# One PSUM tile of three banks for all scores, one minimum and one exponential per head in the even mixer, and norms moved to VectorE

## The chip, the cores and the metric

The kernel runs on one core of a Trainium2 chip. The metric is device time in microseconds (us) for one execution; lower is better. Engines are written as in the profile: PE is TensorE (PEld its weight loads), DVE is VectorE, ACT is ScalarE, POOL is GpSimd, SP is SyncE, whose queue issues most transfers.

## The reference, cut to what matters

The program is two blocks behind each other on 512 tokens of width 1024, all in float32. Block 1 has two layers of latent attention (8 heads, called MLA here) beside a dilated attention, then a norm. Block 2 has an even mixer (attention over 512 own and 256 context keys, beside a multi-scale pool), a hierarchical mixture of 16 experts (moe), an odd mixer and a second moe. The two attentions whose scores the change touches:

```python
# MLA: 8 heads, 4 blocks of 128 queries, 512 keys
s = (qn . k_nope + qr . k_rope) * scale
p = jax.nn.softmax(s, axis=-1)
# even mixer: 8 query heads on 2 key heads, keys = context (256) and own (512)
k_all = jnp.concatenate([kc, k], axis=1)
s = jnp.einsum('bqkgd,bskd->bkgqs', q, k_all) * (HEAD_DIM ** -0.5)
p = jax.nn.softmax(s, axis=-1).astype(v.dtype)
o = jnp.einsum('bkgqs,bskd->bqkgd', p, v_all)
# norms in front of each layer
y = x * rsqrt(mean(x * x) + eps) * g        (block 2: * (1 + scale) + shift)
```

## The kernel before

Float32 products run on PE as three matmuls of a split operand: weights arrive by SP in `wraw` tiles, `split_to` (L403, L404) makes a rounded part `whi` on ACT and a rest `wlo` on DVE, and `mm3` (L352 to L354) issues the three matmuls. All sums land in PSUM, which has eight banks of 128x512 floats. `bank` hands them out as buffers of four tags: `s` (scores, two buffers), `mm` (projections and everything else, three), `pt` (transposes, two) and `av` (values, one). Each buffer is a tile of its own, and the program's builder puts semaphore waits on an instruction by the tiles that it reads and writes.

**Block 1** (span 0 to 955 us, one half for each layer). A layer's order of work is written out by hand: `unit(u)` for u from 0 to 66 issues the scores of unit u (L846 for MLA, 32 units; L825 and L833 for the dilated heads), then the transposes of the probabilities of unit u-2 (L866), and every eighth time the values. `weave` deals a list of fill steps between the units: projections (`fm`, whose sums are taken from PSUM by `block` on ACT, L570 and L574, or by `pair`, L625 and L627, `tile`, L640, and `query`, `key`, L694), gates (`gate`: L650 on ACT, L651 on DVE) and output projections (`wout`, L670 on DVE). For an MLA score DVE takes the row minimum (L848), ACT the exponential with its sum (`softmax`, L805), DVE the reciprocal and the scaling (L807, L808). DVE carries also the columns of the later blocks' modulation (L992, 1.2 us apiece).

**Layer-1 norms** (490 to 515 us): per 128 tokens ACT sums squares (L514), POOL multiplies with the gain (L515), DVE makes the reciprocal root in steps of one column (L386 to L399), ACT scales (L521), PE transposes.

**Even mixer** (955 to 1212 us): after norms and projections 32 units, two per pair of heads and block of 128 queries. `scores(u)` puts 512 own keys in an `s` bank (L1341) and 256 context keys in an `mm` bank (L1343), each as two matmuls; DVE takes two minima and their minimum (L1346 to L1348), ACT two exponentials (L1350, L1351), DVE adds the two sums, takes the reciprocal and scales (L1352 to L1354). `transposed(u-2)` (L1361) turns six pieces through two `pt` banks; `copy` takes turns between ACT (L368, the 512 wide) and DVE (L370, the 256 wide). `values` (L1373) follows every second unit. The fills are pool steps, further queries and the first half of the output projection.

**The moe** (1250 to 1424, 1660 to 1825 us) takes gate and up products of an expert in an `s` bank (`up`, read at L1774 to L1776) and the down product in `mm` banks (L1877, read by DVE at L1879). Its order of instructions is set by the builder's scheduler, not by hand. Behind the first moe come the passages' norms (`added`, L1974 to L1983, and `normed`, L1986), where POOL multiplies for three of four token blocks.

Of the kernel before, what the change touches and what calls it, by code (L numbers as in the profile page):

```python
# [9 lines left out]
F32 = mybir.dt.float32  # L10
# [4 lines left out]
AF = mybir.ActivationFunctionType  # L15
ALU = mybir.AluOpType
AX = mybir.AxisListType
# [4 lines left out]
P = 128  # L22
# [250 lines left out]
class K:  # L273
    def __init__(self, tc, ins, sb, ps, dr):
        self.tc, self.nc, self.I, self.sb, self.ps, self.dr = tc, tc.nc, ins, sb, ps, dr
        self.pool = sb
        self.extra = self.late = None
        self.rate = 0
        self.two = None
        self.tail = None  # L280
        self.of = {}
        self.mod = {}
        self.v4 = ("v4", 10)
        self.n = 0
        self.flip = 0

    def nm(self, s):
        self.n += 1
# [30 lines left out]
            rest(i, a)  # L319
            a, b = b, first(i + 2) if i < 2 else None  # L320

    def bank(self, tag, dt=F32):
        bufs = {"mm": 3, "s": 2, "pt": 2, "av": 1}[tag]
        return self.ps.tile([P, 512], dt, tag=tag, bufs=bufs, name=self.nm("ps" + tag))


    def raw(self, src, off, n):
# [125 lines left out]
def block1_layer(k, L, x, hT):  # L453
# [55 lines left out]
    if L:  # L509
        us, rss = {}, {}  # L510

        def square(i):
            u, ss = us[i], rss[i] = t([P, D], "v4", 10), t([P, 1], "ss", 2)
            nc.scalar.activation(u, x[:, i, :], AF.Square, scale=float(D ** -0.5), accum_out=ss)  # L514
            nc.gpsimd.tensor_tensor(u, x[:, i, :], gB, ALU.mult)  # L515

        def rms_(i):
            return k.rsqrt_steps(rss[i], 1, lambda rs: rss.update({i: rs}))

        def turned(i):  # L520
            nc.scalar.activation(us[i], us[i], AF.Copy, scale=rss[i])  # L521
            return k.norm_steps(us[i], hT, i)

        with k.tc.manual_schedule(engines={ENG.PE, ENG.SP, ENG.Pool, ENG.Activation, ENG.DVE}):
# [616 lines left out]
def even_mixer(k, x, rows):  # L1141
# [45 lines left out]
    nc.sync.dma_start(ic, I["pool_ic"].to_broadcast([P, 64]))  # L1187
    psc = t([P, 4], "psc", 1)
    nc.sync.dma_start(psc, I["psc"])
    for b in range(4):  # L1190
        v.tensor_scalar(psc[:, b : b + 1], psc[:, b : b + 1], 0.5 ** (b + 1), None, op0=ALU.mult)


    T = [t([P, 640], "T", 4) for _ in range(4)]
# [106 lines left out]
        pooled[b] = wp  # L1301

    def pool_mix(b):
        if b % 2 == 0:
            cats[2 + b // 2] = new_cat(k)
        cat = cats[2 + b // 2]
        y = k.bank("mm")
        nc.tensor.matmul(y, pw[:, b * P : (b + 1) * P], pooled[b], start=True, stop=True)
        hi, lo = cat[0][:, b % 2, :], cat[1][:, b % 2, :]
        nc.scalar.activation(hi, y, AF.Copy, scale=psc[:, b : b + 1])  # L1310
        v.scalar_tensor_tensor(lo, y, psc[:, b : b + 1], hi.bitcast(F32), op0=ALU.mult, op1=ALU.subtract)
# [24 lines left out]
    def scores(u):  # L1336
        hp, i, e = u // 8, u % 8 // 2, u % 2
        g, cs = hp // 2, slice(i * P, (i + 1) * P)
        sx, sc = k.bank("s"), k.bank("mm")
        for part in range(2):  # L1340
            nc.tensor.matmul(sx, Qs[(hp, e)][:, cs], Kx[g][part], start=part == 0, stop=part == 1)  # L1341
        for part in range(2):
            nc.tensor.matmul(sc[:, 0:256], Qs[(hp, e)][:, cs], Kc[g][part], start=part == 0, stop=part == 1)  # L1343
        mn = t([P, 3], "mn3", 3)
        l = t([P, 3], "l3", 3)
        v.tensor_reduce(mn[:, 0:1], sx, AX.X, ALU.min)  # L1346
        v.tensor_reduce(mn[:, 1:2], sc[:, 0:256], AX.X, ALU.min)
        v.tensor_tensor(mn[:, 2:3], mn[:, 0:1], mn[:, 1:2], ALU.min)  # L1348
        pr = prs[u] = t([P, 768], "pr", 3)
        nc.scalar.activation(pr[:, 0:512], sx, AF.Exp, scale=-1.0, bias=mn[:, 2:3], accum_out=l[:, 0:1])  # L1350
        nc.scalar.activation(pr[:, 512:768], sc[:, 0:256], AF.Exp, scale=-1.0, bias=mn[:, 2:3], accum_out=l[:, 1:2])  # L1351
        v.tensor_tensor(l[:, 2:3], l[:, 0:1], l[:, 1:2], ALU.add)  # L1352
        v.reciprocal(l[:, 2:3], l[:, 2:3])
        v.tensor_scalar(pr, pr, l[:, 2:3], None, op0=ALU.mult)  # L1354

    def transposed(u):
        PT = PTs[u] = t([P, 6, P], "PT", 4)
        for nk, o in ((4, 0), (2, 4)):
            pt = k.bank("pt")
            for j in range(nk):  # L1360
                nc.tensor.transpose(pt[:, j * P : (j + 1) * P], prs[u][:, (o + j) * P : (o + j + 1) * P], ident)  # L1361
            k.copy(PT[:, o : o + nk, :], pt[:, 0 : nk * P].rearrange("p (j q) -> p j q", j=nk))

    def values(u):

# [4 lines left out]
        for kt in range(6):  # L1370
            vv = V[:, kt, g * 64 : g * 64 + 64] if kt < 4 else ckv[:, kt * P - 256 + g * 64 : kt * P - 192 + g * 64]
            for e in range(2):
                nc.tensor.matmul(k.av[e * 64 : e * 64 + 64, cs], vv, PTs[u - 1 + e][:, kt, :], start=kt == 0, stop=kt == 5)  # L1373
        if i == 3:
            if hp % 2 == 0:
                cats[hp // 2] = new_cat(k, hp == 2)
# [26 lines left out]
    for g in range(2):  # L1403
# [11 lines left out]
        [q(3), mix(2), mix(3)] + wout(3),  # L1415
        wout(0) + [(1.3, lambda: router(k, 0))],
    )
    for w, fill in enumerate(fills):
        n = 8 if w < 3 else 12
        weave([lambda u=u: unit(u) for u in range(8 * w, 8 * w + n)], fill)  # L1420
    k.tail = wout2(k, I["mo"][0], 1, cats[1], x, g1B)


# [105 lines left out]
def moe(k, L, x, tables, out):  # L1529
# [444 lines left out]
    def added(i):  # L1974
# [5 lines left out]
            v.tensor_tensor(x[:, i, ns], acc, x[:, i, ns], ALU.add)  # L1980
            yield
        nc.scalar.activation(t([P, D], "y", 4), x[:, i, :], AF.Square, scale=float(D ** -0.5), accum_out=ss[:, i : i + 1])
        (nc.gpsimd if i else v).tensor_tensor(us[i], x[:, i, :], A1, ALU.mult)  # L1983

    def normed(i):
        v.scalar_tensor_tensor(us[i], us[i], rss[i], sh1, op0=ALU.mult, op1=ALU.add)  # L1986
# [120 lines left out]
```

## Time and profile before

| | us |
|---|---|
| three runs | 1845.24, 1846.01, 1849.75 |
| median | 1846.01 |
| profiled execution | 1847.55 |
| its span | 1845.8 |
| mean granted clock of PE | 0.961 of full speed |
| busy: PE / DVE / ACT / POOL | 1696.8 / 1329.8 / 769.9 / 273.4 |

The profile is of one execution; a row of the timeline gives start, duration, engine, line and operands of an instruction, and in brackets how long its engine had been idle before it and who ended that. Line numbers are those of the kernel before; in the changed kernel the same code stands some lines lower (`mm3` L362 to L364, the MLA score L855, its exponential L814, the transposes L875, the even mixer's scores L1352, its exponential L1357, the moe's down product L1884 and its reader L1886).

### The profile page before, as it was taken

To read this page: it belongs to the slowest core of one execution; us is meant where nothing else is said; L and a number is where in the kernel's file an instruction comes from. 1 tells how busy PE (TensorE), PEld (TensorE's weight loads), DVE (VectorE), ACT (ScalarE), POOL (GpSimd) and SP (SyncE) were. 2 spreads that over 40 slices of the span, in tenths; PEclk is the share of its full clock that TensorE was granted. 3 is DMA by queue.
4 is the path that set the end of the run, shared out by engine and by line. 5 is a ranking of instruction groups with operands and counts; after the bars stand their busy time and mean duration, and the time that the engine had idled before them with its cause. 6 is when DMAs were issued, how large, how long until landed. Compare 5 with 4: busy or idle time off the path is not lost. (4 is left out here: it accounts for less than half of the span.)

```text
span 1845.8 us, 25749 instructions
## 1 busy us (share of the span) xinstructions
PE 1696.8 (92%) x9542; PEld 1325.3 (72%) x9542; DVE 1329.8 (72%) x2519; ACT 769.9 (42%) x1345; POOL 273.4 (15%) x239
## 2 busy tenths in 40 slices
PE   7999999999799999999997888978999799969996
PEld 6877777886697777778776766856665687756663
DVE  5577779876646776566677888889876775589774
ACT  4444333343344533333443545544554322245552
POOL 0000000000200000000003552023221122142221
PEclk9999999999899999999998889988999899979998
DMA  5345565664024455565403223058995553169983
GB/s 177 122 137 159 152 203 179 215 191 127 20 86 121 147 153 149 172 189 154 146 27 111 78 82 115 8 199 295 334 345 145 197 184 92 42 252 308 345 291 75
DMA packets 87588, 300.99 MB, mean 163 GB/s; under 512 B 18982, under 2 KB 20822, under 8 KB 79264
## 3 DMA queue, kind: packets, MB, share of 16 engines
q1 hardware_dynamic: 72224, 273.97, 44.8%
q0 software_dynamic: 10704, 19.79, 4.7%
q10 hardware_dynamic: 4528, 5.51, 1.1%
q8 instruction: 78, 1.28, 0.3%
q14 instruction: 54, 0.44, 0.1%
HBM read 282.33 MB, written 24.96 MB: 166 GB/s over the span
## 5 line engine op out<-in xcount | busy, mean ns | idle before, releaser
L403 ACT ACTIVATE whi<-wraw 128x1024 fp32r<-128x1024 f32 (+2 forms) x166 | 171.8, 1036 | 341.6 <-PE psmm L353 210.8
L404 DVE TENSOR_TENSOR wlo<-wraw,whi 128x1024 fp32r<-128x1024 f32 (+2 forms) x166 | 203.1, 1225 | 104.4 <-ACT whi L403 95.8
L352 PE MATMUL psmm<-big,whi 128*128 128x512 f32 x672 | 271.8, 404 | 1.6 <-ACT e L1289 1.6
L353 PE MATMUL psmm<-big,whi 128*128 128x512 f32 x672 | 265.7, 395 | 0.0
L354 PE MATMUL psmm<-big,wlo 128*128 128x512 f32 x672 | 265.6, 395 | 0.0
L992 DVE CUSTOM_DVE_ANT_0 wraw<-wraw,sB 128x1024 f32<-128x1024 f32 x96 | 116.9, 1221 | 93.8 <-DMA wraw<-in_mw_dram 93.6
L352 PE MATMUL psmm<-whi,big 128*128 128x256 f32 (+2 forms) x496 | 165.6, 334 | 1.0 <-ACT big L403 1.0
L353 PE MATMUL psmm<-wlo,big 128*128 128x256 f32 (+2 forms) x496 | 161.1, 325 | 4.4 <-DVE wlo L404 4.4
L354 PE MATMUL psmm<-whi,big 128*128 128x256 f32 (+2 forms) x496 | 160.2, 323 | 2.5 <-DVE big L404 2.4
L354 PEld LDWEIGHTS psmm<-big,wlo 128*128 128x128 f32 x672 | 126.4, 188 | 30.8
L352 PEld LDWEIGHTS psmm<-big,whi 128*128 128x128 f32 x672 | 126.6, 188 | 29.9 <-ACT e L1289 1.8
L353 PEld LDWEIGHTS psmm<-big,whi 128*128 128x128 f32 x672 | 126.7, 189 | 27.7
L1877 PE MATMUL psmm<-wraw,hs 128*128 128x512 f32 x256 | 122.0, 618 | 5.5 <-ACT hs L1869 3.5
L603 POOL DMA_DIRECT2D qk<-rope x40 | 20.6, 517 | 660.9 <-DVE rope L601 254.1
L353 PEld LDWEIGHTS psmm<-wlo,big 128*128 128x128 f32 x496 | 112.7, 227 | 5.5 <-DVE wlo L404 5.3
L354 PEld LDWEIGHTS psmm<-whi,big 128*128 128x128 f32 x496 | 112.0, 226 | 3.4 <-DVE big L404 3.4
L352 PEld LDWEIGHTS psmm<-whi,big 128*128 128x128 f32 x496 | 112.0, 226 | 2.1 <-ACT big L403 1.6
L352 PE MATMUL pss<-whi,xTh 128*128 128x512 f32 x256 | 104.7, 409 | 2.1 <-ACT xTh L403 2.1
L354 PE MATMUL pss<-whi,xTl 128*128 128x512 f32 x256 | 102.2, 399 | 1.7 <-DVE xTl L404 1.3
L353 PE MATMUL pss<-wlo,xTh 128*128 128x512 f32 x256 | 103.4, 404 | 0.0
L866 PEld LDWEIGHTS pspt<-c_ident,pr 128*128 128x128 f32 x512 | 60.1, 141 | 48.1 <-issue 28.5
L404 DVE TENSOR_TENSOR wlo<-bigm,whi 128x1024 fp32r<-128x1024 f32 x64 | 77.9, 1223 | 17.8 <-ACT whi L403 16.3
(381 smaller groups left out, 3619.1 us busy)
## 6 DMA issues: line engine op xcount, KB each, us to landing
wraw<-in_mw_dram SPq DMA_DIRECT2D x96, 512.0 KB, 3.7
big<-in_me_dram SPq DMA_DIRECT2D x32, 1024.0 KB, 7.9
bigm<-in_me_dram SPq DMA_DIRECT2D x32, 1024.0 KB, 9.2
wraw<-in_me_dram SPq DMA_DIRECT2D x64, 512.0 KB, 8.2
wraw<-in_wqk_dram SPq DMA_DIRECT2D x48, 512.0 KB, 3.9
wraw<-in_wv_dram SPq DMA_DIRECT2D x24, 512.0 KB, 4.6
wraw<-in_ow_dram SPq DMA_DIRECT2D x20, 512.0 KB, 3.7
wraw<-in_wg_dram SPq DMA_DIRECT2D x16, 512.0 KB, 3.9
```

The lines of the kernel that those rows point to most:

```text
L352: mm(out, lhs[0], rhs[0], start=first, stop=False)
L353: mm(out, lhs[0], rhs[1], start=False, stop=False)
L354: mm(out, lhs[1], rhs[0], start=False, stop=last)
L403: self.nc.scalar.activation(hi, src, AF.Copy)
L404: (sub or self.nc.vector).tensor_tensor(lo, src, hi.bitcast(F32), ALU.subtract)
L603: nc.gpsimd.dma_start(tiles[b][48:80, :], R[j][32 * (b % 4) : 32 * (b % 4) + 32, :])
L866: nc.tensor.transpose(pt[:, j * P : (j + 1) * P], hd.pr[i][:, j * P : (j + 1) * P], ident)
L992: nc.vector.tensor_tensor_reduce(w, w, sB, 1.0, 0.0, ALU.mult, ALU.add, mf[:, j : j + 1])
L1877: nc.tensor.matmul(acc, hs[:, c * P : (c + 1) * P], w[:, c * 512 : (c + 1) * 512], start=c == 0, stop=c == 1)
```

## The change

One tile `wide` of three adjacent banks is allocated once and kept for the whole program. `bank("s")` hands out its first and third bank in turn. `bank("mm")` has two buffers of its own and outside the even mixer's units hands out the middle bank of `wide` as every third. In the even mixer's units a pair of heads shares the three banks: the first head has 512 own and 256 context keys in columns 0 to 767, the second 256 context and 512 own keys in columns 768 to 1535, so that one minimum and one exponential of 768 columns serve a head, the adds of partial results go, and the order of the pieces in `values` is rotated for the second head. Both copies of turned probabilities are on ACT. The scaling of `psc` goes into `pool_mix`. The layer-1 norms take one DVE instruction in place of POOL's multiply and ACT's scaling, and the passages' norms multiply on DVE alone.

```diff
--- before.py
+++ after.py
@@ -283,6 +283,8 @@
         self.v4 = ("v4", 10)
         self.n = 0
         self.flip = 0
+        self.wide = ps.tile([P, 3, 512], F32, name="wide")
+        self.turns, self.middle = {"s": 2, "mm": -1}, True
 
     def nm(self, s):
         self.n += 1
@@ -319,9 +321,17 @@
             rest(i, a)
             a, b = b, first(i + 2) if i < 2 else None
 
-    def bank(self, tag, dt=F32):
-        bufs = {"mm": 3, "s": 2, "pt": 2, "av": 1}[tag]
-        return self.ps.tile([P, 512], dt, tag=tag, bufs=bufs, name=self.nm("ps" + tag))
+    def bank(self, tag):
+
+        if tag == "s":
+            self.turns["s"] ^= 2
+            return self.wide[:, self.turns["s"], :]
+        if tag == "mm" and self.middle:
+            self.turns["mm"] = (self.turns["mm"] + 1) % 3
+            if self.turns["mm"] == 2:
+                return self.wide[:, 1, :]
+        bufs = {"mm": 2, "pt": 2, "av": 1}[tag]
+        return self.ps.tile([P, 512], F32, tag=tag, bufs=bufs, name=self.nm("ps" + tag))
 
 
     def raw(self, src, off, n):
@@ -512,13 +522,12 @@
         def square(i):
             u, ss = us[i], rss[i] = t([P, D], "v4", 10), t([P, 1], "ss", 2)
             nc.scalar.activation(u, x[:, i, :], AF.Square, scale=float(D ** -0.5), accum_out=ss)
-            nc.gpsimd.tensor_tensor(u, x[:, i, :], gB, ALU.mult)
 
         def rms_(i):
             return k.rsqrt_steps(rss[i], 1, lambda rs: rss.update({i: rs}))
 
         def turned(i):
-            nc.scalar.activation(us[i], us[i], AF.Copy, scale=rss[i])
+            nc.vector.scalar_tensor_tensor(us[i], x[:, i, :], rss[i], gB, op0=ALU.mult, op1=ALU.mult)
             return k.norm_steps(us[i], hT, i)
 
         with k.tc.manual_schedule(engines={ENG.PE, ENG.SP, ENG.Pool, ENG.Activation, ENG.DVE}):
@@ -1187,8 +1196,6 @@
     nc.sync.dma_start(ic, I["pool_ic"].to_broadcast([P, 64]))
     psc = t([P, 4], "psc", 1)
     nc.sync.dma_start(psc, I["psc"])
-    for b in range(4):
-        v.tensor_scalar(psc[:, b : b + 1], psc[:, b : b + 1], 0.5 ** (b + 1), None, op0=ALU.mult)
 
 
     T = [t([P, 640], "T", 4) for _ in range(4)]
@@ -1301,6 +1308,7 @@
         pooled[b] = wp
 
     def pool_mix(b):
+        v.tensor_scalar(psc[:, b : b + 1], psc[:, b : b + 1], 0.5 ** (b + 1), None, op0=ALU.mult)
         if b % 2 == 0:
             cats[2 + b // 2] = new_cat(k)
         cat = cats[2 + b // 2]
@@ -1336,22 +1344,19 @@
     def scores(u):
         hp, i, e = u // 8, u % 8 // 2, u % 2
         g, cs = hp // 2, slice(i * P, (i + 1) * P)
-        sx, sc = k.bank("s"), k.bank("mm")
-        for part in range(2):
-            nc.tensor.matmul(sx, Qs[(hp, e)][:, cs], Kx[g][part], start=part == 0, stop=part == 1)
-        for part in range(2):
-            nc.tensor.matmul(sc[:, 0:256], Qs[(hp, e)][:, cs], Kc[g][part], start=part == 0, stop=part == 1)
-        mn = t([P, 3], "mn3", 3)
-        l = t([P, 3], "l3", 3)
-        v.tensor_reduce(mn[:, 0:1], sx, AX.X, ALU.min)
-        v.tensor_reduce(mn[:, 1:2], sc[:, 0:256], AX.X, ALU.min)
-        v.tensor_tensor(mn[:, 2:3], mn[:, 0:1], mn[:, 1:2], ALU.min)
+
+        row = k.wide.rearrange("p b n -> p (b n)")
+        sx, sc = row[:, e * 1024 : e * 1024 + 512], row[:, 512 + e * 256 : 768 + e * 256]
+        for out, keys_ in ((sx, Kx), (sc, Kc)):
+            for part in range(2):
+                nc.tensor.matmul(out, Qs[(hp, e)][:, cs], keys_[g][part], start=part == 0, stop=part == 1)
+        src = row[:, e * 768 : e * 768 + 768]
+        mn, l = t([P, 1], "mn3", 3), t([P, 2], "l3", 3)
+        v.tensor_reduce(mn, src, AX.X, ALU.min)
         pr = prs[u] = t([P, 768], "pr", 3)
-        nc.scalar.activation(pr[:, 0:512], sx, AF.Exp, scale=-1.0, bias=mn[:, 2:3], accum_out=l[:, 0:1])
-        nc.scalar.activation(pr[:, 512:768], sc[:, 0:256], AF.Exp, scale=-1.0, bias=mn[:, 2:3], accum_out=l[:, 1:2])
-        v.tensor_tensor(l[:, 2:3], l[:, 0:1], l[:, 1:2], ALU.add)
-        v.reciprocal(l[:, 2:3], l[:, 2:3])
-        v.tensor_scalar(pr, pr, l[:, 2:3], None, op0=ALU.mult)
+        nc.scalar.activation(pr, src, AF.Exp, scale=-1.0, bias=mn, accum_out=l[:, 0:1])
+        v.reciprocal(l[:, 1:2], l[:, 0:1])
+        v.tensor_scalar(pr, pr, l[:, 1:2], None, op0=ALU.mult)
 
     def transposed(u):
         PT = PTs[u] = t([P, 6, P], "PT", 4)
@@ -1359,7 +1364,7 @@
             pt = k.bank("pt")
             for j in range(nk):
                 nc.tensor.transpose(pt[:, j * P : (j + 1) * P], prs[u][:, (o + j) * P : (o + j + 1) * P], ident)
-            k.copy(PT[:, o : o + nk, :], pt[:, 0 : nk * P].rearrange("p (j q) -> p j q", j=nk))
+            nc.scalar.activation(PT[:, o : o + nk, :], pt[:, 0 : nk * P].rearrange("p (j q) -> p j q", j=nk), AF.Copy)
 
     def values(u):
 
@@ -1370,7 +1375,7 @@
         for kt in range(6):
             vv = V[:, kt, g * 64 : g * 64 + 64] if kt < 4 else ckv[:, kt * P - 256 + g * 64 : kt * P - 192 + g * 64]
             for e in range(2):
-                nc.tensor.matmul(k.av[e * 64 : e * 64 + 64, cs], vv, PTs[u - 1 + e][:, kt, :], start=kt == 0, stop=kt == 5)
+                nc.tensor.matmul(k.av[e * 64 : e * 64 + 64, cs], vv, PTs[u - 1 + e][:, (kt + 2 * e) % 6, :], start=kt == 0, stop=kt == 5)
         if i == 3:
             if hp % 2 == 0:
                 cats[hp // 2] = new_cat(k, hp == 2)
@@ -1415,9 +1420,11 @@
         [q(3), mix(2), mix(3)] + wout(3),
         wout(0) + [(1.3, lambda: router(k, 0))],
     )
+    k.middle = False
     for w, fill in enumerate(fills):
         n = 8 if w < 3 else 12
         weave([lambda u=u: unit(u) for u in range(8 * w, 8 * w + n)], fill)
+    k.middle = True
     k.tail = wout2(k, I["mo"][0], 1, cats[1], x, g1B)
 
 
@@ -1980,7 +1987,7 @@
             v.tensor_tensor(x[:, i, ns], acc, x[:, i, ns], ALU.add)
             yield
         nc.scalar.activation(t([P, D], "y", 4), x[:, i, :], AF.Square, scale=float(D ** -0.5), accum_out=ss[:, i : i + 1])
-        (nc.gpsimd if i else v).tensor_tensor(us[i], x[:, i, :], A1, ALU.mult)
+        v.tensor_tensor(us[i], x[:, i, :], A1, ALU.mult)
 
     def normed(i):
         v.scalar_tensor_tensor(us[i], us[i], rss[i], sh1, op0=ALU.mult, op1=ALU.add)
```

Three places show how the built program's PE rows change. Behind a row in brackets stand the engines on whose semaphores it waits; `wide` is the new tile, `pss`, `psmm`, `pspt` buffers of the tags, `pr` probabilities.

PE in block 1, an MLA score, the transposes of the unit two before it, and the first product of a fill step; before:

```order
L846 MATMUL pss_1044<-qk_815,qk_801 128x512 [waits Activation_49]
L866 MATMUL pspt_1053<-c_ident,pr_948 128x128 [waits DVE_49,PE_49]
L866 MATMUL pspt_1053<-c_ident,pr_948 128x128 x3
L352 MATMUL psmm_1059<-whi_993,big_77 128x256
L353 MATMUL psmm_1059<-wlo_994,big_77 128x256
L354 MATMUL psmm_1059<-whi_993,big_78 128x256
```

and now:

```order
L855 MATMUL wide<-qk_808,qk_794 128x512 [waits Activation_49]
L875 MATMUL pspt_1038<-c_ident,pr_935 128x128 [waits PE_49]
L875 MATMUL pspt_1038<-c_ident,pr_935 128x128 x3
L362 MATMUL wide<-whi_979,big_78 128x256 [waits Activation_49]
L363 MATMUL wide<-wlo_980,big_78 128x256
L364 MATMUL wide<-whi_979,big_79 128x256
```

The order of the rows stays, but the fill step's first product, which goes to the middle bank and waited for nothing, now waits for ACT.

PE in the even mixer, the scores of units 0 and 1 and, behind a fill step, of unit 2; before:

```order
L1341 MATMUL pss_9658<-Kx_9519,Q_9549 128x512 [waits DVE_49,Activation_49]
L1341 MATMUL pss_9658<-Kx_9520,Q_9549 128x512 [waits DVE_49]
L1343 MATMUL psmm_9659<-Kc_9513,Q_9549 128x256
L1343 MATMUL psmm_9659<-Kc_9514,Q_9549 128x256
L1341 MATMUL pss_9675<-Kx_9519,Q_9552 128x512 [waits DVE_49]
L1341 MATMUL pss_9675<-Kx_9520,Q_9552 128x512
L1343 MATMUL psmm_9676<-Kc_9513,Q_9552 128x256
L1343 MATMUL psmm_9676<-Kc_9514,Q_9552 128x256
...
L1341 MATMUL pss_9735<-Kx_9519,Q_9549 128x512 [waits Activation_49]
L1341 MATMUL pss_9735<-Kx_9520,Q_9549 128x512
L1343 MATMUL psmm_9736<-Kc_9513,Q_9549 128x256 [waits Activation_49]
L1343 MATMUL psmm_9736<-Kc_9514,Q_9549 128x256
```

and now:

```order
L1352 MATMUL wide<-Kx_9304,Q_9334 128x512 [waits DVE_49,Activation_49]
L1352 MATMUL wide<-Kx_9305,Q_9334 128x512 [waits DVE_49]
L1352 MATMUL wide<-Kc_9298,Q_9334 128x256
L1352 MATMUL wide<-Kc_9299,Q_9334 128x256
L1352 MATMUL wide<-Kx_9304,Q_9337 128x512 [waits Activation_49]
L1352 MATMUL wide<-Kx_9305,Q_9337 128x512
L1352 MATMUL wide<-Kc_9298,Q_9337 128x256
L1352 MATMUL wide<-Kc_9299,Q_9337 128x256
...
L1352 MATMUL wide<-Kx_9304,Q_9334 128x512 [waits Activation_49]
L1352 MATMUL wide<-Kx_9305,Q_9334 128x512
L1352 MATMUL wide<-Kc_9298,Q_9334 128x256
L1352 MATMUL wide<-Kc_9299,Q_9334 128x256
```

The scores of units 0 and 1 waited apart for engines that had prepared their operands; now unit 1 waits for ACT, and behind the fill step one wait stands for the three banks.

PE in the first moe, in its steady part: turned inputs of an expert (L1759, now L1766), down products (L1877, now L1884), turned hidden values (L1867, now L1874) and the first gate and up product of the next expert (L352, now L362); before:

```order
L1867 MATMUL pspt_12519<-c_ident,pr_12427 128x128
L1759 MATMUL pspt_12545<-c_ident,xg_11252 128x128 [waits DMASW2_49,PE_49]
L1759 MATMUL pspt_12545<-c_ident,xg_11252 128x128 x3
L1877 MATMUL psmm_12529<-wraw_12525,hs_12522 128x512 [waits DMAHW1_49,Activation_49]
L1877 MATMUL psmm_12529<-wraw_12525,hs_12522 128x512
L1877 MATMUL psmm_12533<-wraw_12526,hs_12522 128x512 [waits DMAHW2_49]
L1877 MATMUL psmm_12533<-wraw_12526,hs_12522 128x512
L1759 MATMUL pspt_12552<-c_ident,xg_11252 128x128 [waits PE_49]
L1759 MATMUL pspt_12552<-c_ident,xg_11252 128x128 x3
L352 MATMUL pss_12559<-whi_12563,xTh_12543 128x512 [waits Activation_49]
```

and now:

```order
L1766 MATMUL pspt_12034<-c_ident,xg_10847 128x128 [waits DMASW1_49,PE_49]
L1766 MATMUL pspt_12034<-c_ident,xg_10847 128x128 x3
L1884 MATMUL psmm_12022<-wraw_12016,hs_12012 128x512 [waits DMAHW6_49,Activation_49]
L1884 MATMUL psmm_12022<-wraw_12016,hs_12012 128x512
L1884 MATMUL wide<-wraw_12015,hs_12012 128x512 [waits DMAHW5_49,DVE_49]
L1884 MATMUL wide<-wraw_12015,hs_12012 128x512
L1766 MATMUL pspt_12041<-c_ident,xg_10847 128x128 [waits PE_49]
L1766 MATMUL pspt_12041<-c_ident,xg_10847 128x128 x3
L1874 MATMUL pspt_12095<-c_ident,pr_12005 128x128 [waits DVE_49,PE_49]
L1874 MATMUL pspt_12095<-c_ident,pr_12005 128x128
L362 MATMUL wide<-whi_12051,xTh_12032 128x512 [waits DVE_49,Activation_49]
```

The transposes of the hidden values come ahead of the next expert's products instead of behind them, and both the second down product and those products wait for DVE.

## Rows read from the trace of the kernel before

**Rows 1.** Windows: busy us (instructions) by engine, PE's clock, DMA share, GB/s.

```profile
90.00:250.00 160.00, 158.89 (x735) 118.52 (x734) 115.75 (x210) 67.37 (x129) 3.27 (x6) 1.00 0.51 149
...
1057.00:1100.00 43.00, 34.09 (x176) 26.98 (x175) 36.58 (x73) 18.82 (x45) 25.21 (x22) 0.80 0.14 40
1100.00:1150.00 50.00, 44.84 (x309) 35.34 (x307) 41.11 (x94) 27.54 (x65) 14.54 (x10) 0.97 0.34 122
1250.00:1424.00 174.00, 167.35 (x738) 115.02 (x738) 144.21 (x203) 93.06 (x128) 42.91 (x29) 0.98 0.85 292
```

**Rows 2.** Timeline around an MLA score at 111.6: start, duration, engine, line, operands.

```profile
111.62 1.02 PE L846 MATMUL pss<-qk,qk 96*128 96x512 f32 x2
...
111.95 1.21 DVE L992 CUSTOM_DVE_ANT_0 wraw<-wraw,sB 128x1024 f32<-128x1024 f32 x1
...
112.84 0.36 PE L352 MATMUL psmm<-whi,big 128*128 128x256 f32 x1
...
113.47 0.69 DVE L848 TENSOR_REDUCE mn<-pss 128x1 f32<-128x512 f32 x1
...
114.26 0.69 ACT L805 ACTIVATE pr<-pss,mn 128x512 f32<-128x512 f32 x1 [0.54 <-DVE mn L848]
```

**Rows 3.** Timeline around the first MLA score: the score and the gate's last reader.

```profile
92.89 1.02 PE L846 MATMUL pss<-qk,qk 96*128 96x512 f32 x2
...
95.06 0.69 DVE L651 SCALAR_TENSOR_TENSOR gc<-gc,psmm 128x512 f32<-128x512 f32 x1
```

**Rows 4.** Timeline around a dilated score: the score and the copy that reads a projection.

```profile
919.78 0.66 PE L825 MATMUL pss<-k,qk 64*32 64x256 f32 x16
...
920.61 0.58 ACT L571 ACTIVATE k<-psmm 128x512 f32<-128x512 f32 x1
```

**Rows 5.** Line L574, copies of a projection: duration ns min/median/max.

```profile
L574 ACT ACTIVATE qk<-psmm x40: 571/578/598, 165.5 to 914.6; 128x512 f32<-128x512 f32 x40
```

**Rows 6.** Groups, 1054 to 1210: busy us, mean ns, idle before and releaser.

```profile
L1350 ACT ACTIVATE pr<-pss,mn 128x512 f32<-128x512 f32 x32 | 22.0, 686 | 32.6 <-DVE mn L1348 29.0 <-DVE rs_yn L399 2.8 <-DVE PT L370 0.8
L1346 DVE TENSOR_REDUCE mn<-pss 128x1 f32<-128x512 f32 x32 | 21.9, 683 | 7.9 <-PE pss L1341 7.8
...
L1351 ACT ACTIVATE pr<-psmm,mn 128x256 f32<-128x256 f32 x32 | 14.9, 465 | 0.0
...
L1352 DVE TENSOR_TENSOR l<-l 128x1 f32<-128x1 f32 x32 | 13.3, 416 | 7.0 <-ACT pr L1351 6.6
L1347 DVE TENSOR_REDUCE mn<-psmm 128x1 f32<-128x256 f32 x32 | 13.3, 414 | 0.0
L370 DVE COPY PT<-pspt 128x256 f32<-128x256 f32 x32 | 13.2, 414 | 0.2
...
L1348 DVE TENSOR_TENSOR mn<-mn 128x1 f32<-128x1 f32 x32 | 8.1, 252 | 0.0
```

**Rows 7.** Timeline of the layer-1 norms: POOL's multiply and root steps.

```profile
490.25 2.40 POOL L515 TENSOR_TENSOR v<-x,v 128x1024 f32<-128x1024 f32 x1 [44.66 <-ACT v L514]
...
491.10 1.56 DVE L393 SCALAR_TENSOR_TENSOR rs_u<-rs_y,rs_h 128x1 f32<-128x1 f32 x1
...
493.38 0.21 DVE L393 SCALAR_TENSOR_TENSOR rs_u<-rs_y,rs_h 128x1 f32<-128x1 f32 x1
```

**Rows 8.** Timeline in the first moe: a down product's reader and PE's next product.

```profile
1308.51 0.75 DVE L1879 SCALAR_TENSOR_TENSOR y<-psmm,ws,mv 128x512 f32<-128x512 f32 x1 [0.31 <-PE psmm L1877]
...
1308.66 0.47 PE L352 MATMUL pss<-whi,xTh 128*128 128x512 f32 x1
```

**Rows 9.** Windows around two gaps on PE, at 1586 and 307.

```profile
1585.00:1588.50 3.50, 1.65 (x8) 1.03 (x7) 2.99 (x2) 0.00 (x0) 2.44 (x1) 1.00 0.00 0
1588.50:1591.90 3.40, 3.40 (x10) 2.62 (x9) 1.98 (x3) 0.00 (x0) 0.00 (x0) 0.50 0.00 0
306.00:309.40 3.40, 1.50 (x7) 0.96 (x6) 3.37 (x6) 0.00 (x0) 0.00 (x0) 1.00 0.90 305
309.40:312.80 3.40, 3.25 (x15) 2.33 (x15) 3.40 (x10) 1.63 (x4) 0.00 (x0) 1.00 0.55 167
```

## The prediction

> **What bounds the kernel now.** I read the windows by stage first, then the timeline where the changed PE rows stand, then the groups of the even mixer. In the MLA stretch of layer 0 PE is busy 158.89 of 160 us at full clock, DVE 115.75 and ACT 67.37 [rows 1]; layer 1's stretch (580 to 740 us) reads the same. So block 1 is bound by PE: any time that PE waits there is added to the end, and anything that DVE or ACT saves there is worth nothing. The first moe is alike (PE 167.35 of 174). Only the start of the even mixer's attention is not: from 1057 to 1100 PE has 34.09 of 43 us at a mean clock of 0.80, and DVE, with 36.58, is the fuller engine; from 1100 to 1150 PE has 44.84 of 50 [rows 1].
>
> **The change, part by part.** The profiled execution took 1847.55 us, 1.54 above the median of the three runs; the sum is made against 1847.55.
>
> *The new waits in block 1.* The rows of the built program show that its waits are set by tile, and `wide` is one tile. A product in its middle bank therefore waits until the last reader of a score in an outer bank is done, and a score in an outer bank until the last reader of a projection in the middle one is done, though they touch other columns. What that costs is read from the trace as it stands. At 111.62 PE starts an MLA score of 1.02 us, and at 112.84 the fill step's first product, free of any wait [rows 2]. In the changed program this product (L362) waits for the exponential of that very score: counting ACT's completions up to the one that the wait names ends at it. DVE is at other work (L992 until 113.16, and a scaling), so the minimum starts at 113.47, and the exponential ends at 114.26 + 0.69 = 114.95 [rows 2]. PE would stand for 114.95 - 112.84 = 2.11 us. With DVE and ACT free it would be 111.62 + 1.02 + 0.69 + 0.69 + 0.13 for the hand-overs - 112.84 = 1.31 us. Behind the waiting row stand PE's next 24 matmuls and all later transposes, so DVE and ACT get their next work as much later; nothing runs past it on PE. The other direction: the first MLA score starts at 92.89, while the gate that lies in the middle bank is read until 95.06 + 0.69 = 95.75, 2.86 us later [rows 3]. A dilated score at 919.78 meets a copy that ends at 920.61 + 0.58, 1.41 us later [rows 4].
>
> I did this for every PE row of block 1 that now waits for a reader of other columns. There are 104; for 68 the reader ends after the row's start in the trace:
>
> - exponential of a score (L805): 64 waits, 36 late, 63.6 us as the trace stands; 36.3 us with empty queues (30 at about 1.2 us)
> - copy of a projection (L574, 0.578 us [rows 5]): 12 waits, 10 late, 14.5 and 7.9 us
> - gate (L650, L651): 4 waits, all late, 11.7 and 6.4 us
> - the other readers (L570, L625, L627, L640, L670, L694): 24 waits, 18 late, 22.3 and 12.2 us
>
> Sum 112.1 and 62.8 us. These are the two ends: when PE stands, DVE's and ACT's queues run down, so the later waits come out shorter than in the trace; but DVE keeps its 116 us of work per MLA stretch, so the queues do not vanish. I take **+85**, a little under half way from the empty queues: DVE's share falls from 72% to 116 of about 203 us, 57%, and the queueing part (49 us) I take as a bit less than halved.
>
> *The same in the moe and the odd mixer.* A down product lies in the middle bank and is read by L1879; the next expert's first product now waits for it: 1308.51 + 0.75 - 1308.66 = 0.60 us [rows 8]. There are 47 waits of this and the like kind in both moes, 20 late, 18.9 us as they stand, 15.4 with empty queues; the odd mixer has two late ones, 2.7 us. **+22**, from 10 to 44: the scheduler has put the moe's rows in another order, whose effect no row shows, so I allow half or double.
>
> *The even mixer.* Per unit DVE loses 0.683 + 0.414 + 0.252 + 0.416 of minima and adds and 0.414 of copies, 2.179 us [rows 6]. The minimum of 768 columns that comes instead is not in the trace. From 256 to 512 columns it grows by 0.269, so 0.952 by the same slope; it is at least 0.683 and at most 0.683 + 0.414. That frees 32 x 1.227 = 39 us of DVE. ACT's exponential goes from 0.686 + 0.465 to 0.686 + 0.221 = 0.907 and a second copy comes, taken at 0.44 between L370's 0.414 and L1351's 0.465 for the same size; ACT is about even, and its 18.82 of 43 us leave room [rows 1, 6]. But PE is idle for only 8.9 + 5.2 = 14.1 us in the two windows, so that is all there is to win. Against it, unit u's scores now wait for the exponential of unit u-1 and not u-2. In 10 of 31 units PE has less between them than 0.952 + 0.907 and hand-overs, 6.4 us in all with empty queues, about 13 with DVE's queue as it is. Net **-3**, from -12 to +12. What is late next there is the exponential. The scaling of `psc` (four instructions of one column) and the rotated order cost nothing: they lie behind work that waits for PE.
>
> *The norms.* While POOL multiplies for 2.40 us, a root step on DVE takes 1.56 instead of 0.21 [rows 7]; four such in layer 1 and three behind the first moe stretch by some 1.3 to 2 us each, in places where PE waits for the norm. POOL's multiplies go; in their place are DVE instructions of 128x1024, about 1.2 us by L992's size [rows 2]. **-5**, from -10 to 0.
>
> *The clock.* PE loses some 115 us to stalls of 0.6 to 3 us. Around 1586 PE was idle for 1.85 of 3.5 us, and the next 3.4 us ran at 0.50, the lower of the two levels; around 307 it was idle for 1.90 of 3.4 us and the next stretch kept 1.00 [rows 9]. So a stall of two microseconds can bring the clock down or not. Each such stretch costs 1.7 us of PE work; I take nine, **+15**, from 0 to 45.
>
> Sum: 85 + 22 - 3 - 5 + 15 = +114, 1847.55 + 114 = **1962 us**.
>
> **The rivals.**
>
> *Faster, about 1826.* The attention is where the gain decides: if DVE's 39 us came out in full on PE's idle time there (-12) and the norms gave -10, with the new waits covered, the time would be 1826. This holds only while the waits on `wide` cost under 22 us, 0.2 us for each of block 1's 104. For it speaks DVE's 36.58 of 43 us from 1057 to 1100; against it that PE in block 1 runs 1 to 2 us behind a score's start while its exponential ends 3.3 us behind it [rows 1, 2]. 3 in 100.
>
> *No waits across banks, about 1840 to 1846.* In the trace PE fills one bank while DVE takes the minimum of another, at 113.47 [rows 2], so a wait across banks serves nothing on the chip. If the program needed waits only inside a bank, block 1 and the moe would cost nothing and the attention would keep its own shared bank: 1847.55 - 3 - 5 = 1840, or 1846 if the shared bank takes 6 us. The Trainium skill ("PSUM — Partial Sum Buffer", section Terms) gives collisions as a matter of bank and 32-partition quadrant, not of a whole tensor, so by that rule this is the outcome. The rows of the built program speak against it: L362 has no wait before and one on ACT now, for a bank that no one else uses. 4 in 100, half of it faster and half the same.
>
> *The clock falls throughout the MLA stretches, about 2007.* With the stalls PE's busy share in them comes to 159 of some 200 us, which is that of the window from 1057 to 1100 (34.09 of 43), where the mean clock is 0.80 [rows 1]. At 0.80 the 159 us become 199, which partly fills the stalls; between 20 and 40 us for each of the two layers, 60 in place of the 15. For it speaks that equal share; against it that these stalls are short and even, while those before 1100 come in lumps. 16 in 100.
>
> **How the numbers follow.** The forecast, with waits between their two ends, has 75 in 100; 2 in 100 are left for mishaps without a sign of their own, counted as slower. Its own bounds are 63 + 10 - 12 - 10 + 0 = +51 and 112 + 44 + 12 + 0 + 45 = +213, all ends at once. Eight in ten should lie from **1900** (+52) to **2040** (+192), which takes in the clock rival and leaves out the two fast ones. Under 0.3% (5.5 us) a run of this kernel can't be told from no change. Faster: 3 + 2 = 5 in 100; the same: 2; slower: 75 + 16 + 2 = 93.
>
> **What would show it.** PE's waits in the MLA stretches, now 1.1 us, should name ACT's exponential before L362 and L855 in first place, with 40 to 65 us in all, and the gate and copies with some 20; the two layers should be longer by 30 to 55 us each. In the moe L362 should wait about 0.6 us for L1886 once in most experts. The minimum of 768 columns should take 0.9 to 1.1 us, and the stretch from 1057 to 1210 should change by less than 12 us. The layer-1 root steps should all be near 0.2 us. The prediction is wrong if PE still starts its middle-bank products while a score's exponential runs, or if block 1 ends near 955 us.

## The result, and the profile after

The changed kernel takes 1993.55 us (median of four runs, 1992.95 to 1995.96) against 1847.16 for the kernel before on the same chip: a ratio of 1.079, 95% interval 1.0774 to 1.0806. It is 146 us slower. Forecast were 1962 us, from 1900 to 2040.

The windows of four stages of block 1, of the even mixer's attention and of the two moes tell where the time went. Their borders are the same PE rows in both kernels (first and last score of a stage, first turned input and last or next product of a moe); columns as in [rows 1]. Before:

```profile
92.89:246.51 153.62, 152.51 (x705) 113.52 (x704) 112.81 (x205) 63.84 (x124) 3.27 (x6) 1.00 0.51 150
246.51:470.27 223.76, 217.43 (x1474) 171.81 (x1472) 172.43 (x334) 84.71 (x148) 11.16 (x24) 1.00 0.57 179
581.06:734.10 153.04, 152.15 (x705) 112.91 (x704) 112.06 (x203) 67.50 (x128) 3.01 (x6) 1.00 0.51 147
734.10:953.37 219.27, 217.51 (x1473) 171.75 (x1472) 143.49 (x290) 81.12 (x144) 10.52 (x23) 1.00 0.49 147
1057.42:1199.38 141.96, 126.54 (x855) 102.94 (x853) 117.72 (x276) 72.98 (x180) 39.67 (x31) 0.92 0.20 67
1250.15:1430.13 179.98, 172.66 (x749) 117.19 (x749) 145.02 (x204) 94.08 (x130) 44.31 (x30) 0.97 0.83 283
1652.64:1832.28 179.64, 173.50 (x748) 116.54 (x748) 139.02 (x194) 91.48 (x126) 45.78 (x30) 0.98 0.83 277
```

and after:

```profile
97.34:306.36 209.02, 172.09 (x704) 121.94 (x705) 117.62 (x206) 66.75 (x126) 3.27 (x6) 0.92 0.40 115
306.36:540.79 234.43, 218.58 (x1474) 173.33 (x1472) 171.36 (x328) 82.37 (x144) 11.22 (x24) 0.99 0.55 166
655.06:862.35 207.29, 173.14 (x704) 122.77 (x705) 114.33 (x199) 67.02 (x127) 2.98 (x6) 0.92 0.37 108
862.35:1091.89 229.54, 218.29 (x1473) 173.15 (x1472) 144.39 (x289) 80.19 (x143) 10.32 (x23) 0.99 0.47 141
1199.22:1343.93 144.71, 127.73 (x853) 101.93 (x854) 98.96 (x153) 70.96 (x146) 35.39 (x30) 0.93 0.20 65
1395.84:1578.95 183.11, 172.82 (x748) 117.02 (x749) 143.22 (x204) 95.08 (x130) 43.52 (x29) 0.98 0.83 281
1794.38:1979.14 184.76, 174.57 (x747) 117.50 (x748) 141.03 (x196) 92.57 (x127) 43.72 (x30) 0.98 0.82 269
```

The two MLA stretches grow by 55.4 and 54.3 us, the two dilated ones by 10.7 and 10.3: 130.6 of the 146. In each row the length less PE's busy time is PE's idle time. Over the four stretches it goes from 10.1 to 98.2 us, so **88 us are waits**. The other **42.5 us are longer matmuls**: in an MLA stretch the same 705 take 172 us in place of 152, and the granted clock falls from 1.00 to 0.92 (the lower level is 0.50, so 16% of the stretch, some 33 us in each layer, ran there). By the clock's own records, 69 us of PE's busy time in the four stretches lie in pieces at 0.50; at 1.00 they would be half as long, so the lower clock is **35 of the 42.5 us**. What lengthens the rest, 8 us, is not settled. The attention is 2.8 us longer although DVE has 19 us less to do, and the moes 3.1 and 5.1.

What PE waited for up to 1092 us, by the waits view (total, times, longest):

```profile
PE wide L362 <- ACT pr L814: 35.0, 20, 2.9
PE wide L855 <- ACT pr L814: 14.8, 10, 2.2
PE wide L855 <- DVE gc L660: 11.5, 4, 3.4
PE wide L362 <- DVE mn L864: 11.3, 4, 5.4
...
PE wide L834 <- ACT qk L583: 8.4, 6, 1.4
...
PE wide L855 <- ACT qk L583: 5.6, 4, 1.4
```

All rows of this view that begin with `wide` come to 104 us. Of these 98 lie inside the four stretches, where they are all of PE's idle time, and 6 just ahead of the first MLA score of each layer. The first row is the wait of [rows 2]. Here is that place in the timeline after:

```profile
121.24 1.02 PE L855 MATMUL wide<-qk,qk 96*128 96x512 f32 x2
...
121.70 1.23 DVE L1001 CUSTOM_DVE_ANT_0 wraw<-wraw,sB 128x1024 f32<-128x1024 f32 x1
...
122.86 0.68 DVE L857 TENSOR_REDUCE mn<-wide 128x1 f32<-128x512 f32 x1
123.63 0.69 ACT L814 ACTIVATE pr<-wide,mn 128x512 f32<-128x512 f32 x1 [0.30 <-DVE mn L857]
...
124.47 0.38 PE L362 MATMUL wide<-whi,big 128*128 128x256 f32 x1 [1.76 <-ACT pr L814]
```

The product starts 3.23 us behind the score's start instead of 1.22, when the exponential of that score, in another bank, has ended (124.32). It stood for 1.76 us by the row, between the 2.11 and the 1.31 that were worked out.

### The profile page after: what moved, and what is told of

Its sections match the earlier page's. It is cut to its first block, busy times and chain, and to the rows that moved or that the text cites. A ratio compares the mean times of both kernels' runs of the same rounds, so it can differ in the third digit from the quotient of the medians.

```text
span 1992.3 us, 25597 instructions
## 1 busy us (share of the span) xinstructions
PE 1741.5 (87%) x9542; PEld 1345.8 (68%) x9542; DVE 1321.2 (66%) x2398; ACT 769.5 (39%) x1309; POOL 254.7 (13%) x232
## 3 DMA queue, kind: packets, MB, share of 16 engines
q8 instruction: 78, 1.28, 0.3%
## 5 line engine op out<-in xcount | busy, mean ns | idle before, releaser
L414 DVE TENSOR_TENSOR wlo<-wraw,whi 128x1024 fp32r<-128x1024 f32 (+2 forms) x166 | 203.4, 1226 | 137.6 <-ACT whi L413 128.3
L362 PE MATMUL psmm<-big,whi 128*128 128x512 f32 x464 | 187.7, 404 | 0.0
L364 PE MATMUL psmm<-big,wlo 128*128 128x512 f32 x464 | 183.7, 396 | 0.0
L363 PE MATMUL psmm<-big,whi 128*128 128x512 f32 x464 | 183.7, 396 | 0.0
L362 PE MATMUL wide<-whi,xTh 128*128 128x512 f32 x256 | 107.9, 422 | 6.9 <-DVE pr L1783 3.7
L362 PE MATMUL psmm<-whi,big 128*128 128x256 f32 (+2 forms) x332 | 109.4, 329 | 1.1 <-ACT big L413 1.1
L855 PE MATMUL wide<-qk,qk 96*128 96x512 f32 x128 | 73.1, 654 | 42.0 <-ACT pr L814 14.8
L364 PE MATMUL psmm<-whi,big 128*128 128x256 f32 (+2 forms) x332 | 106.0, 320 | 0.3 <-DVE big L414 0.3
L364 PE MATMUL wide<-whi,xTl 128*128 128x512 f32 x256 | 102.7, 401 | 1.7 <-DVE xTl L414 1.7
L363 PE MATMUL wide<-wlo,xTh 128*128 128x512 f32 x256 | 102.4, 400 | 0.0
L362 PEld LDWEIGHTS psmm<-big,whi 128*128 128x128 f32 x464 | 87.6, 189 | 19.4 <-issue 0.4
L363 PEld LDWEIGHTS psmm<-big,whi 128*128 128x128 f32 x464 | 87.6, 189 | 19.1
L362 PE MATMUL wide<-big,whi 128*128 128x512 f32 x208 | 88.6, 426 | 11.6 <-ACT pr L814 11.6
L875 PEld LDWEIGHTS pspt<-c_ident,pr 128*128 128x128 f32 x512 | 62.6, 145 | 49.8 <-issue 34.2
L414 DVE TENSOR_TENSOR wlo<-bigm,whi 128x1024 fp32r<-128x1024 f32 x64 | 78.4, 1225 | 24.5 <-ACT whi L413 22.3
L414 DVE TENSOR_TENSOR wlo<-big,whi 128x1024 fp32r<-128x1024 f32 x58 | 70.8, 1225 | 25.8 <-ACT whi L413 24.3
L363 PE MATMUL wide<-big,whi 128*128 128x512 f32 x208 | 86.7, 417 | 0.0
```

Of the source, the lines that this page charges most:

```text
L362: mm(out, lhs[0], rhs[0], start=first, stop=False)
L363: mm(out, lhs[0], rhs[1], start=False, stop=False)
L364: mm(out, lhs[1], rhs[0], start=False, stop=last)
L414: (sub or self.nc.vector).tensor_tensor(lo, src, hi.bitcast(F32), ALU.subtract)
L855: nc.tensor.matmul(sp, q[:, i * P : (i + 1) * P], kt, start=True, stop=True)
L875: nc.tensor.transpose(pt[:, j * P : (j + 1) * P], hd.pr[i][:, j * P : (j + 1) * P], ident)
```

## The experiments

Each is timed in turns with the kernel before on one chip; ratios are to that, with 95% intervals.

**Sharing alone, and the same rotation in three tiles.** e1 gives the kernel before only the new `bank`, e2 the same with a tile for each bank:

```diff
+        self.wide = ps.tile([P, 3, 512], F32, name="wide")          # e1
+        self.wide = [ps.tile([P, 512], F32, name=f"wide{j}") for j in range(3)]   # e2
```

> The kernel before with nothing but the bank sharing: scores and every third mm buffer lie in one tile of three banks, the even mixer's scores still in two pieces, norms and copies as before. Theory (the cost is the tile-wide waits): block 1 again 135 to 140 us longer, the moes some 8 us, in all 1985 to 2005. Rival (the cost is in the rest of the change, the copies on ACT or the norms on DVE): 1841 to 1853.

> As e1, the same rotation by hand of the same three banks, but each bank a tile of its own. Theory (it is the tile's size, not the rotation): no new waits, 1841 to 1853. Rival (buffers kept for the whole program and rotated by hand cost by themselves): above 1900, near e1.

e1 took 2050.73 us (1.110, 1.1082 to 1.1119), e2 1848.50 (1.0012, 0.9996 to 1.0028). PE's waits in the MLA stretch of e2, 90 to 250 us, are no more than the 1.1 us of before:

```profile
PE wide L856 <- DMA qk<-krT: 0.4, 1, 0.4
PE psmm L364 <- DVE wlo L414: 0.3, 1, 0.3
```

So the waits come from one thing, that three banks are one tile (PE's matmuls stand in the same order in e1 and e2 to the end of the even mixer; only behind it has the scheduler put e1's in another); the rotation, the buffers kept for the whole program and their assignment cost nothing that these runs can tell from zero. The Trainium skill ("PSUM — Partial Sum Buffer", section Summary) says to guard reads of PSUM beside matmuls by bank; e2 does just that, and its time is that of the kernel before. e1 came out above its range: its stages to the end of block 1 are like the changed kernel's, but the attention is 49 us longer than before, since scores in two pieces, fill steps and the output projection all wait in one tile there. The changed kernel avoids that: its fill steps do not use the middle bank in the units, and one exponential frees all of a head's columns.

**The rest of the change without the wide tile.**

> The changed kernel with the banks and the even mixer's scores of before: the copies on ACT, the scaling of psc and both moves of norms stay. Theory: the norms behind the first moe give what after showed from the spread to the second router, about 8 us, the layer-1 norms 0 to 4; 1835 to 1845. Rival (the rest of the change costs too): 1850 to 1860.

e3 took 1838.63 us (0.9954, 0.9937 to 0.9971): 8 us faster than before, the lowest median of all kernels run here (e7's, 1839.84, can't be told from it). The rest of the change is a gain.

**The wide tile in the even mixer alone.** A pool of three banks is closed and opened around the units:

```diff
-    k.middle = False
+    k.banks(False)      # closes s, s, mm; opens wide
...
-    k.middle = True
+    k.banks(True)
```

> The changed kernel, with the tile of three banks opened for the even mixer's units alone; everywhere else scores and mm buffers are tiles of one bank. Theory: block 1 and the moes at the time of before, norms 8 us faster, the attention between 10 us faster and 5 us slower by the tile-wide waits among its own units: 1828 to 1848. Rival (the wide scores lose in the attention itself): 1850 or more, with PE's waits on the exponential (L1357 in the changed kernel) above 10 us.

e4 took 1846.31 us (1.0002, 0.9990 to 1.0014), inside the theory's range. Block 1 and the moes are at the time of before, as the theory has it; but e4 is 7.7 us slower than e3, and the waits that the rival named came, so in its direction the rival was right. In the two profiles, which are 3.4 us apart, the attention makes 2.2 of that. PE's waits from 1060 to 1212 in e4:

```profile
PE wide L1356 <- ACT pr L1361: 13.5, 15, 4.1
PE pspt L1370 <- ACT PT L1371: 2.4, 3, 0.9
PE wide L1356 <- ACT e L1300: 2.0, 1, 2.0
```

In 15 of 31 units the scores wait for the exponential of the unit before, 13.5 us in all, as in the changed kernel (13.4). The third row is the first score, waiting for the last reader of a buffer that stood in those banks.

**A tile for each head.** Two tiles of two banks in turn, so that unit u waits for unit u-2 again; mm has one bank there:

```diff
-        row = k.wide.rearrange("p b n -> p (b n)")
+        row = k.own.tile([P, 2, 512], F32, tag="pair", bufs=2, ...).rearrange("p b n -> p (b n)")
```

> As e4, but in the even mixer's units each head's 768 columns lie in a tile of two banks of its own, two such tiles in turn, which leaves one mm bank for the fill steps. Theory (in e4 the one minimum and exponential are worth several us, taken back by unit u waiting for unit u-1): without that wait the attention gets 5 to 12 us shorter than e3's 139.7, 1828 to 1836. Rival (the attention is not bound by DVE's minima, or one mm bank costs as much): 1838 to 1850.

e6 took 1846.13 us (1.0000, 0.9982 to 1.0018), in the rival's range. Its waits from 1061 to 1210:

```profile
PE pspt L1369 <- ACT PT L1370: 7.9, 8, 3.0
PE psmm L365 <- DVE cbtl L1322: 3.1, 2, 1.6
PE pair L1355 <- ACT e L1299: 2.9, 1, 2.9
```

The wait on exponentials is gone. The transposes wait for ACT's copies, 9.1 us in all where e3 has 6.1, and two fill steps for DVE's reader of the one mm bank, 3.1 us where e3 has 2.2. The attention takes 139.1 us between its first and last score, e3 139.7, though DVE is busy for 96.7 us instead of 114.4: the one minimum and one exponential are worth next to nothing here, even without their wait. What else makes e6 7.5 us longer than e3 in the runs is not settled; in the two profiles it is spread over stages before and behind the attention.

**Norms or copies.**

```diff
-        (nc.gpsimd if i else v).tensor_tensor(us[i], x[:, i, :], A1, ALU.mult)      # e7, with L515 and L521
+        v.tensor_tensor(us[i], x[:, i, :], A1, ALU.mult)
-            k.copy(PT[:, o : o + nk, :], pt...)                                      # e8
+            nc.scalar.activation(PT[:, o : o + nk, :], pt..., AF.Copy)
```

> The kernel before with both moves of norms and nothing else. Theory (the gain of e3, 8 us, is the norms'): 1836 to 1842. Rival (it is the copies on ACT): 1844 to 1850.

> The kernel before with both turned copies of the even mixer on ACT and nothing else. Theory (the norms give e3's gain): 1843 to 1849. Rival: 1836 to 1842.

e7 took 1839.84 us (0.9967, 0.9951 to 0.9982), e8 1843.85 (0.9983, 0.9970 to 0.9996). The norms carry most of e3's gain and the copies a smaller part, if any; the sum, 9.6 us, agrees with e3's 8.2 within the intervals.

**Does the standing pull the clock down?** Idle transposes fill the stalls:

```diff
                 if self.fresh is not None:
+                    junk = self.ps.tile([P, 512], F32, tag="av", bufs=1, ...)
+                    for j in range(12):
+                        self.nc.tensor.transpose(junk[...], self.fresh[...], self.ident)
```

> The changed kernel with 12 idle transposes of 128x128 (about 0.11 us each, into a bank nobody reads) ahead of a middle-bank product, in 27 places of the MLA stretches; in 18 of them the product waits for the exponential of a score. They add no wait, and run in time that PE stood still. Theory (the stalls themselves pull the clock down): PE's time at half clock in the two MLA stretches, 68 us in the changed kernel, falls to 45 or less, worth 11 us or more; the 9 fills without a stall cost 12 us at most, so 1980 to 1995. Rival (the clock falls for another reason, and the stalls only coincide): half-clock time stays at 60 to 75 us and the time rises to 2000 to 2010.

e5 took 1986.66 us (1.0752, 1.0734 to 1.0770), 7 us less than the changed kernel with 240 matmuls more; the fills stand in 20 places, not 27, of which 18 are ahead of a waiting product. Its MLA stretches:

```profile
96.80:297.50 200.70, 172.62 (x813) 126.38 (x814) 117.62 (x206) 66.83 (x126) 3.27 (x6) 0.98 0.41 120
649.70:853.60 203.90, 178.57 (x813) 130.55 (x814) 114.05 (x199) 67.23 (x127) 2.98 (x6) 0.95 0.38 110
```

The clock goes from 0.92 to 0.98 and 0.95. By the same reading as above (the mean clock of each stretch), time at half clock falls from 67 to 28 us; PE idles 53.4 us instead of 71.1, and the stretches are 11.7 us shorter. So the lower clock follows from PE standing, and is a second price of the same waits. The fills do not shorten the wait of a score for an exponential: in the MLA stretch of layer 0 that row (L862 <- L821 in e5, L855 <- L814 in the changed kernel) stays at 7.9 us.

**Which banks may share.** e9 puts only the two score banks of the kernel before in one tile; e10 leaves the middle bank of the changed kernel unused outside the units:

```diff
+        self.both, self.side = ps.tile([P, 2, 512], F32, name="both"), 1     # e9
-        self.turns, self.middle = {"s": 2, "mm": -1}, True                   # e10
+        self.turns, self.middle = {"s": 2, "mm": -1}, False
```

> The kernel before with nothing but its two score banks in one tile of two; the three mm buffers stay tiles of their own. Theory (a wait comes wherever two banks of one tile are used in turn, and costs what the chain minimum, exponential lacks to the next score): in the MLA stretches a score that starts before the exponential of the one before it has ended waits; in the trace of before these are 20 scores, 24 us as it stands and 12 with empty queues, plus some 10 us of clock and a few us in the attention: 1865 to 1895. Rival (the cost is in scores and projections sharing a tile, and scores alone are spaced far enough): 1843 to 1855.

> The changed kernel with the middle bank left unused outside the even mixer's units, so that mm has two buffers everywhere and only scores lie in the wide tile. Theory: the waits between scores alone, as e9, less some 8 us of the norms, and little for the third mm buffer: 1858 to 1895, over two thirds of the 146 us back. Rival (projections need three buffers): above 1900, with PE's waits before products of psmm on DVE or ACT readers above 20 us.

e9 took 1904.90 us (1.0320, 1.0291 to 1.0349), e10 1906.98 (1.0341, 1.0303 to 1.0379), 10 and 12 us above the theory's ranges. e10's time lies in its rival's range, and the rival's sign came too: PE's waits before `psmm` products for readers of a buffer are some 30 us by the rows (9 in the kernel before), over the 20 that it named. Waits of PE in e9 and then in e10, whole span:

```profile
PE both L1345 <- ACT pr L1354: 24.3, 15, 8.6
PE both L850 <- ACT pr L809: 22.1, 12, 3.0
```

```profile
PE wide L855 <- ACT pr L814: 22.6, 12, 3.1
...
PE wide L1352 <- ACT pr L1357: 15.2, 14, 7.1
PE psmm L362 <- DVE ss L1179: 15.2, 1, 15.2
```

In block 1 the theory's size holds: 22 us of waits between scores in either, between the 12 and 24 expected. With the lower clock that comes with them (0.96 and 0.97) the two MLA stretches are 37 us longer in e9 and 38 in e10. What was too small is the rest. In e9 scores in two pieces wait 24.3 us in the attention, where I had allowed a few. In e10 one product waits 15.2 us in the norms ahead of the even mixer, and the stretch between block 1 and the first even score is 9 us longer than before. The row names L1179; the reader of the product's mm buffer is L679, just ahead of it on DVE:

```profile
1031.89 0.21 DVE L1311 TENSOR_SCALAR psc<-psc 128x1 f32<-128x1 f32 x2 [7.93 <-DMA psc<-in_psc_dram]
...
1037.87 2.19 DVE L1176 SCALAR_TENSOR_TENSOR ss<-ss 128x1 f32<-128x1 f32 x1
...
1040.17 0.68 DVE L679 TENSOR_TENSOR x<-psmm,x 128x512 f32<-128x512 f32 x1
...
1040.90 0.58 PE L362 MATMUL psmm<-whi,v 128*128 128x256 f32 x1 [15.22 <-DVE ss L1179]
```

That reader stood behind 7.93 us in which DVE waited for a transfer (5.7 in the kernel before) and behind two one-column steps of over 2 us. So scores that share a tile among themselves cost 22 us in waits over the two layers, and the third mm buffer had kept PE clear of DVE's queue in that one place, where its lack costs some 9; by difference, scores and projections that share the tile cost the rest of block 1's 88.

## Why the prediction was right, point by point

*What bounds, and the waits of block 1* (+85, from 63 to 112): PE was idle 88 us more, so the term held, and the choice a little under half way between empty queues and the trace's own. That 85 came out so near is in part luck, since its parts differ more. The exponentials cost 35.0 + 14.8 = 49.8 us (36 to 64 expected), the copies by L583 14.0 (8 to 14.5), the gates 11.5 (6.4 to 11.7), all inside their ends. The list lacked a reader: four middle-bank products beside dilated scores waited 11.3 us for the masked minimum of a score (L864), and the other readers came out at about 14 instead of 12 to 22, which made up for a part of that. That the waits are set by the tile is shown by e1 against e2, whose code differs in nothing else.

*The clock* (+15, from 0 to 45): this is the term that was mis-sized. In the four stretches PE needed 42.5 us more for the same matmuls, 35 of it by the clock, inside the range but more than twice the 15. I had taken nine stretches of 3.4 us at half clock, 31 us; the MLA stretches alone spent 67 us there. The rival that took the fall for the whole MLA (60 us, mean clock 0.80) went too far, as the clock came out at 0.92; but the measured time is 13 us from its 2007 and 32 from the forecast's 1962. Its reason was right in kind, and e5 shows it: the stalls cause it.

*The moes and the odd mixer* (+22, from 10 to 44): mis-sized the other way. The moes grew by 8.2 us. The wait of [rows 8] is there, but small; PE's waits in the first moe after:

```profile
PE wide L1884 <- DVE pr L1783: 2.6, 4, 1.3
PE wide L362 <- DVE pr L1783: 2.0, 1, 2.0
...
PE wide L362 <- DVE y L1886: 1.1, 4, 0.3
```

The forecast had 0.60 us for most experts from L1886; it is 0.3 in four. The order of the built program showed a likely reason, and I gave it no value: the transposes of the next hidden values (L1874) now stand between the down products and L362 and can fill that time. That the scheduler's new order by itself costs nothing was not tried apart from the tile.

*The even mixer* (-3, from -12 to +12): +2.8 between its first and last score. The two new durations came out as worked out by the slope:

```profile
L1355 DVE TENSOR_REDUCE mn<-wide 128x1 f32<-128x768 f32 x32 | 30.6, 955 | 13.3 <-PE wide L1352 13.1
L1357 ACT ACTIVATE pr<-wide,mn 128x768 f32<-128x768 f32 x32 | 28.9, 904 | 14.1 <-DVE mn L1355 14.0
...
L1352 PE MATMUL wide<-Kx,Q 128*128 128x512 f32 x64 | 23.4, 448 | 16.1 <-ACT pr L1357 13.4 <-ACT e L1296 2.6
```

0.955 against 0.952, and 0.904 against 0.907 us. The wait for the unit before, 13.4 us, is at the upper figure of the forecast (6.4 to 13). The 39 us that DVE was to be freed of became 19 in the stage (the windows above). The sum of 2.179 us a unit added durations that overlap; in the kernel before, L1347 starts ahead of L1346's end:

```profile
1123.23 0.68 DVE L1346 TENSOR_REDUCE mn<-pss 128x1 f32<-128x512 f32 x1
1123.82 0.41 DVE L1347 TENSOR_REDUCE mn<-psmm 128x1 f32<-128x256 f32 x1
```

The durations of all DVE rows of the stage sum to 134.9 us before and 103.2 after, 32 less, but to 117.7 and 99.0 us of busy time: an instruction that goes takes its overlap with it. And e6 shows that even without the wait DVE's relief brings next to nothing: it was not on PE's path.

*The norms* (-5, from -10 to 0): e7 gives -6.8, 95% interval -9.0 to -3.3. In the changed kernel the stretch between the two moes, which holds the passages' norms and the odd mixer, is 7.1 us shorter. The layer-1 root steps are level, as said (min/median/max in ns; before, the largest was 2.19 us and [rows 7] has one of 1.56):

```profile
L403 DVE SCALAR_TENSOR_TENSOR rs_u<-rs_y,rs_h x12: 209/220/221, 562.2 to 576.6; 128x1 f32<-128x1 f32 x12
```

In the changed kernel itself the stretch from the last dilated score to layer 1's first MLA score is still 3.5 us longer than before, as it ends with a score that waits 3.4 us for a gate (L855 <- L660).

*The rivals.* Faster by the attention needed waits under 22 us; they were 104. The rule by bank was decided by the builder, as its rows had shown; the kernel that follows it, e2, runs at the time of before. The sum came out 32 us short of the measured time: too little by 28 for PE's longer matmuls (20 of it clock), by 3 for the waits, by 6 for the attention and by ten for all that lies outside the seven stretches, against 14 too much for the moes and the odd mixer.

## What to carry to other kernels

Before one PSUM tile is made to span several banks, read in the built program's order which rows of PE have gained a wait: in this program a semaphore set by the tile couples readers and writers of banks that never meet, and where PE is the full engine each such row costs the rest of the reader's chain (here minimum and exponential, 1.2 to 2.9 us where a fill step waited). Give the stage that needs adjacent banks its own tile and leave the others a tile per bank; then check that the stage gains at all, since an engine's relief counts only where PE waits for it. And price a row of stalls twice, once as time and once as clock.

## What was not expected of the hardware

Matmuls without use, twelve in each of 20 places, most of them where PE would have stood, made the kernel 7 us faster: time at the lower clock level fell from 67 to 28 us in the MLA stretches. And in the attention the stretching of DVE instructions beside POOL's did not go with the one-column adds, which had taken 0.416 us in the mean [rows 6]. Other DVE instructions in the same stage became longer: L414's 128x1024 form took 1.44 us in the mean where before it had 1.28, and two of three root steps (L409) over 2.2 us, where before all three had 0.17. The first of the two beside POOL's multiply:

```profile
1204.74 2.35 POOL L350 TENSOR_TENSOR wraw<-wraw,e 128x1024 f32<-128x1024 f32 x1 [2.33 <-DVE mn L1355]
...
1204.84 2.28 DVE L409 SCALAR_TENSOR_TENSOR rs_yn<-rs_un,rs_yn 128x16 f32<-128x16 f32 x1
```

This is a smaller part of why DVE's 39 us became 19; the larger is the overlap told above.
